# Top-10 indices of 8192 rows: each row spread over 16 partitions, sums of exponentials folded across partitions by one-hot matmuls, and candidates gathered as single columns

## The chip, the cores and the metric

One core of one Trainium2 chip. The metric is the time of one execution in device microseconds (us); medians of several executions are given. Trace views are of one profiled execution each. Lines such as L124 are lines of the kernel in question, so they differ between the two kernels. In the views PE is TensorE, PEld its weight loads, DVE VectorE, ACT ScalarE and POOL GpSimd; SPq and ACTq are the queues on which SyncE and ScalarE issue DMA transfers. PEclk is the TensorE clock that was granted; clock 1.00 is called warm below, 0.50 cold.

## The reference, cut to what matters

```python
def setup_inputs():
    return {"x": np.random.randn(8192, 8192).astype(np.float32), "k": 10}

def reference(x, k):
    indices = np.argpartition(x, -k, axis=1)[:, -k:]
    values = np.take_along_axis(x, indices, axis=1)
    sorted_idx = np.argsort(-values, axis=1)
    return np.take_along_axis(indices, sorted_idx, axis=1)
```

The input is 8192 x 8192 x 4 bytes = 268.4 MB. The output is small: ten 64-bit indices a row.

## The kernel before

The kernel takes 128 rows at a time (a tile; 64 of them). ScalarE computes steep exponentials of the whole row, TensorE adds them up over chunks of eight neighbouring elements, VectorE finds the twelve chunks with the largest sums, GpSimd gathers the elements of those chunks, TensorE sorts the gathered pieces to their rows, and VectorE ranks the 96 candidates. A final check falls back to a slow exact branch if the twelve chunks could have missed something.

```python
C = 8; NCHUNK = N // C; G = 12; PER = 6; HALF = NCHUNK // 2; LAG = 2     # (cut)

def load(t):                     # partition p holds row t*128 + p; 2 pieces of 16 KB a partition (8 of 4 KB for tile 0)
    ...
def weigh(t):
    for h in range(2):
        e = epool.tile([P, HALF, C], bf16, tag="e", name="e")
        nc.scalar.activation(out=e..., in_=xt[:, h * H:(h + 1) * H], func=ACTF.Exp, ...)
        for w in range(C):
            nc.tensor.matmul(ss[t][:, h, :], lhsT=eye, rhs=e[:, :, w],     # every eighth bf16
                             start=w == 0, stop=w == C - 1)

def choose(t):                   # max / max_index / match_replace / max / max_index over 1024 sums, then the indices
    ...
def gather(t):
    for a in range(G // PER):    # two instructions; 16 x 6 indices each, a run of 8 elements per index
        runs = gws[t][:, :, a * PER:(a + 1) * PER, :].rearrange("p r s w -> p s r w")
        nc.gpsimd.add_instruction(mybir.InstIndirectCopy(..., num_valid_indices=16 * PER))

def extract(t):                  # each partition's own row out of the 16 rows gathered in its group
    for r in range(16):
        nc.tensor.matmul(gs[t], lhsT=own[:, r, :], rhs=gw[:, r, :, :]..., start=r == 0, stop=r == 15)

# (cut) schedule: weigh(0), weigh(1); then per t: choose(t), gather(t), weigh(t+2), extract(t), load(t+3), rank(t-2)
```

A GpSimd gather applies the same list of indices to a whole group of 16 partitions: the trace shows it writing 128x768, 96 runs of 8 elements in every partition, of which six are its own row's. In this kernel the 16 partitions hold 16 different rows, so of every run that is gathered only one partition in 16 holds something that is wanted, and the matmuls with masked identities throw the rest away.

## Time and profile before

| | before |
|---|---|
| median time | 1342.99 us |
| TensorE busy | 1309.0 us (98%) |
| of a tile's 20.5 us: chunk sums / extraction | 14.4 / 6.1 us |
| GpSimd per tile, two gathers | 4.8 us for one; 9.8 us from when the indices are ready to when the extraction may start |
| loads | 268.4 MB at a mean of 202 GB/s |

The lines that carry this stand in the prediction. Two more rows of the page, each with one value for each fortieth of the span, show the granted TensorE clock in tenths and the rate of the DMA engines:

```profile
PEclk9956556566565565565665655655656656556556
...
GB/s 396 315 231 218 229 156 244 208 168 251 184 194 250 163 213 235 159 235 212 165 250 191 188 250 164 214 236 156 235 213 166 251 189 187 251 151 227 126 0 3
```

The DMA row starts near 400 GB/s while the first buffers fill and then sinks to about 200, because each load waits for a buffer that TensorE's pace sets free (SyncE's queue waits 1059.7 us, 60 times, for the gather that ends a buffer's use, and the gather waits for the sums). This is what a hidden transfer looks like: it could go twice as fast.

### The profile page before, as it was taken

The page shows a single profiled execution, that of the slowest core. Times are in us where ns is not written, and L with a number is a line of the kernel's source. Part 1 is how long each engine was busy: PE and PEld are TensorE (multiplying, and loading weights), DVE is VectorE, ACT ScalarE, POOL GpSimd, SP SyncE. Part 2 cuts the span into 40 slices and gives each one's busy share as a digit, 9 for nine tenths or more (in the row PEclk, how much of TensorE's full clock was granted, in tenths as well). Part 3 has the DMA queues.
Part 4 walks back from the last instruction along what each step waited for, and adds up shares of the span by engine and source line. Part 5 has one row for each costly group of instructions (what it writes and reads, how often), then busy time and mean ns, then how long its engine had stood idle before and what let it go on. Part 6 is the DMA issues. An engine that isn't in the chain of part 4 may idle for free.

```text
span 1341.3 us, 8449 instructions
## 1 busy us (share of the span) xinstructions
PE 1309.0 (98%) x3074; PEld 526.6 (39%) x3074; DVE 527.7 (39%) x1208; ACT 488.2 (36%) x258; POOL 147.0 (11%) x135
## 2 busy tenths in 40 slices
PE   5999999999999999999999999999999999999995
PEld 0234434434344344344343343442443433434424
DVE  0524325334254244343353342542434433434424
ACT  5433433433334334334334333343343343333410
POOL 0111110110111111101101101111111011011110
PEclk9956556566565565565665655655656656556556
DMA  9755546546446455455465464554554644645300
GB/s 396 315 231 218 229 156 244 208 168 251 184 194 250 163 213 235 159 235 212 165 250 191 188 250 164 214 236 156 235 213 166 251 189 187 251 151 227 126 0 3
DMA packets 27945, 270.75 MB, mean 202 GB/s; under 512 B 10496, under 2 KB 10624, under 8 KB 11648
## 3 DMA queue, kind: packets, MB, share of 16 engines
q1 hardware_dynamic: 27616, 269.10, 50.1%
q10 hardware_dynamic: 288, 1.11, 0.2%
q8 instruction: 24, 0.39, 0.1%
q14 instruction: 17, 0.14, 0.0%
HBM read 269.55 MB, written 0.66 MB: 201 GB/s over the span
## 4 chain that ended last, share of the span: by engine, by line
PE 98%; DMA 1%; issue 0%; ACT 0%; DVE 0%; POOL 0%; SPq 0%; ACTq 0%
PE s L124 69%; PE g L168 29%; DMA xt<-in_x_dram 1%; ACT e L118 0%; POOL gw L154 0%; ACT L118 0%; SPq L80 0%; DVE hot L198 0%; DVE hot L202 0%; DVE posb L182 0%; DVE posb L179 0%; DVE pick L206 0%; DVE t8a L178 0%; DVE t8b L181 0%; DVE ngood L245 0%
## 5 line engine op out<-in xcount | busy, mean ns | idle before, releaser
L124 PE MATMUL s<-e,eye 128*128 128x512 bf16 x1024 | 931.6, 1077 | 16.3 <-ACT e L118 16.3
L118 ACT ACTIVATE e<-xt,bias 128x4096 bf16<-128x4096 f32 x128 | 474.7, 3708 | 786.1 <-issue 779.4
L168 PEld LDWEIGHTS g<-gw,own 128*128 128x128 f32 x2048 | 407.1, 304 | 91.5 <-issue 84.5
L124 PEld LDWEIGHTS <-eye 128*128 128x128 bf16 x1024 | 125.9, 124 | 713.8 <-issue 709.4
L168 PE MATMUL g<-gw,own 128*128 128x96 f32 x2048 | 398.3, 387 | 6.8 <-POOL gw L154 6.8
L136 DVE MAX8 wall<-s 128x8 f32<-128x1024 f32 x64 | 78.9, 1233 | 770.8 <-PE s L124 770.8
L154 POOL INDIRECT_COPY gw<-xt,idx 128x768 f32 x128 | 146.3, 1143 | 1177.6 <-issue 1010.2
L141 DVE MAX8 wall<-m 128x8 f32<-128x1024 f32 x64 | 78.6, 1228 | 2.2
L137 DVE FIND_INDEX8 cidb<-wall,s 128x8 uint16<-128x1024 f32 x64 | 78.3, 1223 | 0.0
L142 DVE FIND_INDEX8 cidb<-wall,m 128x8 uint16<-128x1024 f32 x64 | 78.0, 1219 | 0.0
L139 DVE MATCH_REPLACE8 m<-wall,s 128x1024 f32<-128x1024 f32 x64 | 77.7, 1214 | 0.0
L118 ACT ACTIVATION_READ_ACCUMULATOR e<-xt,bias 128x1 f32 x128 | 23.9, 186 | 0.0
L178 DVE MAX8 t8a<-g 128x8 f32<-128x96 f32 x64 | 16.6, 259 | 13.4 <-PE g L168 13.4
L234 ACT ACTIVATE e<-tall,bias 128x64 f32<-128x64 f32 x1 | 0.3, 348 | 48.5 <-DVE tall L183 48.5
L181 DVE MAX8 t8b<-g 128x8 f32<-128x96 f32 x64 | 16.7, 261 | 2.2
L179 DVE FIND_INDEX8 posb<-t8a,g 128x8 uint16<-128x96 f32 x64 | 16.4, 257 | 0.0
L182 DVE FIND_INDEX8 posb<-t8b,g 128x8 uint16<-128x96 f32 x64 | 16.1, 252 | 0.0
L180 DVE MATCH_REPLACE8 g<-t8a,g 128x96 f32<-128x96 f32 x64 | 15.8, 247 | 0.0
L144 DVE TENSOR_SCALAR idx<-cidb 128x12 uint16<-128x12 uint16 x64 | 10.9, 171 | 7.4 <-DVE cidb L142 0.9
L198 DVE TENSOR_TENSOR hot<-slot,slots 128x960 f16<-128x960 uint16 x8 | 9.3, 1167 | 0.0
L206 DVE TENSOR_REDUCE pick<-hot 128x80 f32<-128x960 f16 x8 | 9.2, 1152 | 0.2
L183 DVE COPY tall<-t8b 128x1 f32<-128x1 f32 x64 | 8.6, 134 | 0.0
(27 smaller groups left out, 47.9 us busy)
## 6 DMA issues: line engine op xcount, KB each, us to landing
xt<-in_x_dram SPq DMA_DIRECT2D x126, 2048.0 KB, 11.7
xt<-in_x_dram SPq DMA_DIRECT2D x8, 512.0 KB, 9.2
own<-topk_own ACTq DMA_DIRECT2D x1, 1024.0 KB, 7.2
out_dram<-opack SPq DMA_DIRECT2D x8, 80.0 KB, 3.1
eye_f<-topk_eye ACTq DMA_DIRECT2D x1, 64.0 KB, 3.3
```

Source lines behind the costliest of these rows:

```text
L118: nc.scalar.activation(out=e.rearrange("p c w -> p (c w)"), in_=xt[:, h * H:(h + 1) * H], func=ACTF.Exp, bias=bias[:, 0:1], scale=BETA, ac ...
L124: nc.tensor.matmul(ss[t][:, h, :], lhsT=eye, rhs=e[:, :, w], start=w == 0, stop=w == C - 1)
L136: nc.vector.max(out=w16[:, 0:8], in_=m)
L137: nc.vector.max_index(out=cid[:, 0:8], in_max=w16[:, 0:8], in_values=m)
L139: nc.vector.match_replace(out=m2, in_to_replace=w16[:, 0:8], in_values=m, imm_value=-1.0)
L141: nc.vector.max(out=w16[:, 8:16], in_=m2)
L142: nc.vector.max_index(out=cid[:, 8:16], in_max=w16[:, 8:16], in_values=m2)
L154: nc.gpsimd.add_instruction(mybir.InstIndirectCopy(name=nc.get_next_instruction_name(), ins=[nc.gpsimd.lower_ap(xts[t]), nc.gpsimd.lower_a ...
L168: nc.tensor.matmul(gs[t], lhsT=own[:, r, :], rhs=gw[:, r, :, :].rearrange("p s w -> p (s w)"), start=r == 0, stop=r == 15)
L178: nc.vector.max(out=t8a, in_=g)
L179: nc.vector.max_index(out=pos[:, 0:8], in_max=t8a, in_values=g)
L181: nc.vector.max(out=t8b, in_=g2)
```

## The change

The intent is to read the exponentials in the order in which they lie. A row is cut into 16 parts of 512 elements which lie in 16 neighbouring partitions; a chunk is then one column of 16 elements, one in each of those partitions. Sums across partitions are what a matmul does: sixteen one-hot weight tiles (`group`) fold the parts of eight rows each into the 128 output rows. A gather of one index now brings 16 wanted elements, one in each partition. They arrive in the wrong direction, so each gathered column is multiplied with a mask (`spread`) and turned back by a matmul (`extract`). The core of the diff, with cuts marked:

```diff
-        for w in range(C):
-            nc.tensor.matmul(ss[t][:, h, :], lhsT=eye, rhs=e[:, :, w], start=w == 0, stop=w == C - 1)
+        for i in range(SP_):
+            s = h * SP_ + i
+            nc.tensor.matmul(ss[t], lhsT=group[:, s, :], rhs=e[:, i, :], start=s == 0, stop=s == S - 1)
 # ... load: 2 KB runs instead of rows
+        src = x[t * P:(t + 1) * P, :].rearrange("(s a) (q j) -> (a q) s j", a=A, q=R)
+        for s in range(0, S, S // 4):
+            nc.sync.dma_start(out=dst[:, s:s + S // 4, :], in_=src[:, s:s + S // 4, :])
 # ... choose over 512 sums instead of 1024; one gather of 16 x 12 single elements instead of two of 16 x 6 runs of 8
+    def spread(t):
+        nc.vector.tensor_tensor(out=masked[t], in0=cands.pop(t)..., in1=own..., op=ALU.mult)     # 128 x 1536
     def extract(t):
-        for r in range(16): nc.tensor.matmul(gs[t], lhsT=own[:, r, :], rhs=gw[:, r, :, :]..., ...)
+        for c in range(G):
+            nc.tensor.matmul(gs[t][:, c, :], lhsT=mk[:, c, :, :]..., rhs=place, start=True, stop=True)
 # ... rank over 192 candidates instead of 96, its six steps interleaved with the six of choose; LAG 3
+    def store(b):                # results of 8 tiles: eight stores from ScalarE's queue (before: one from SyncE's)
+        for a in range(A):
+            nc.scalar.dma_start(out=out_atn[a, :, b * TB:(b + 1) * TB, :], in_=o[a * S:(a + 1) * S, :, :])
 # ... schedule per t: choose(t) with rank(t-3), gather(t), weigh(t+1), store, spread(t-1), extract(t-1), decode, load(t+3)
```

More of the change, by code (lines that the diff above doesn't have):

```diff
@@ L12 @@
 N = 8192
-C = 8
-NCHUNK = N // C
+R = 16
+A = P // R
+S = P // A
+W = N // R
 KMAX = 10
 G = 12
-PER = 6
-HALF = NCHUNK // 2
+PIECES = 2
+SP_ = S // PIECES
 TB = 8
@@ L24 @@
 BIG_NEG = -1e30
-LAG = 2
+LAG = 3
 @with_exitstack
@@ L52 @@
     out_u32 = out.bitcast(u32)
-    out_tpn = out_u32.rearrange("(t p) n -> p t n", p=P)
+    out_atn = out_u32.rearrange("(t s a) n -> a s t n", s=S, a=A)
     consts = ctx.enter_context(tc.tile_pool(name="consts", bufs=1))
     epool = ctx.enter_context(tc.tile_pool(name="e", bufs=3))
-    gwpool = ctx.enter_context(tc.tile_pool(name="gw", bufs=2))
     small = ctx.enter_context(tc.tile_pool(name="small", bufs=2))
@@ L64 @@
     gpsum = ctx.enter_context(
-        tc.tile_pool(name="gpsum", bufs=2, space=bass.MemoryType.PSUM)
+        tc.tile_pool(name="gpsum", bufs=3, space=bass.MemoryType.PSUM)
     )
@@ L69 @@
     )
-    xts, es, ss, gs, idxs, gws, batch = {}, {}, {}, {}, {}, {}, {}
-    H = N // 2
+    xts, ss, gs, idxs, cands, masked, batch, ready = {}, {}, {}, {}, {}, {}, {}, {}
     def load(t):
         xts[t] = xpool.tile([P, N], fp32, tag="xt", name="xt")
-        r0 = t * P
-        nparts = 8 if t == 0 else 2
-        w = N // nparts
-        for h in range(nparts):
-            nc.sync.dma_start(
-                out=xts[t][:, h * w:(h + 1) * w], in_=x[r0:r0 + P, h * w:(h + 1) * w]
-            )
+        src = x[t * P:(t + 1) * P, :].rearrange("(s a) (q j) -> (a q) s j", a=A, q=R)
+        dst = xts[t].rearrange("p (s j) -> p s j", j=W)
+        n = S // 4
+        for s in range(0, S, n):
+            nc.sync.dma_start(out=dst[:, s:s + n, :], in_=src[:, s:s + n, :])
     for t in range(3):
         load(t)
+    part = np.arange(P)
+    own_np = (part[:, None] // R == np.arange(A)[None, :]).astype(np.float32)
+    place_np = (part[:, None] % R == np.arange(R)[None, :]).astype(np.float32)
+    base_np = ((part % S) * W).astype(np.float32)[:, None]
+    cpack_np = np.concatenate([own_np, place_np, base_np], axis=1)
+    cpack_dram = nc.inline_tensor(np.ascontiguousarray(cpack_np), name="topk_cpack")
+    cpack = consts.tile([P, A + R + 1], fp32)
+    nc.scalar.dma_start(out=cpack, in_=cpack_dram.ap())
+    own, place, base = cpack[:, 0:A], cpack[:, A:A + R], cpack[:, A + R:A + R + 1]
     bias = consts.tile([P, 1], fp32)
@@ L90 @@
     nc.vector.memset(ones, 1.0)
-    eye_np = np.eye(P, dtype=np.float32)
-    eye_dram = nc.inline_tensor(eye_np, name="topk_eye")
-    eye_f = consts.tile([P, P], fp32)
-    nc.scalar.dma_start(out=eye_f, in_=eye_dram.ap())
-    eye = consts.tile([P, P], bf16)
-    nc.vector.tensor_copy(out=eye, in_=eye_f)
-    own_np = np.stack([np.diag((np.arange(P) % 16 == r).astype(np.float32)) for r in range(16)], 1)
-    own_dram = nc.inline_tensor(np.ascontiguousarray(own_np).reshape(P, 16 * P), name="topk_own")
-    own = consts.tile([P, 16, P], fp32)
-    nc.scalar.dma_start(out=own.rearrange("p r q -> p (r q)"), in_=own_dram.ap())
+    group = consts.tile([P, S, P], bf16)
+    nc.vector.memset(group, 0.0)
+    for s in range(S):
+        nc.vector.tensor_copy(
+            out=group[:, s, :].rearrange("p (a s) -> p a s", s=S)[:, :, s], in_=own
+        )
     slots_i = consts.tile([P, G], i32)
@@ L107 @@
     tall = consts.tile([P, ntiles], fp32)
-    eall = consts.tile([P, ntiles, 2], fp32)
+    eall = consts.tile([P, ntiles, PIECES], fp32)
     opacks = [consts.tile([P, TB, KMAX, 2], u32, name=f"opack{i}") for i in range(2)]
@@ L114, in weigh @@
         xt = xts[t]
-        ss[t] = spsum.tile([P, 2, HALF], fp32, tag="s", name="s")
-        for h in range(2):
-            e = epool.tile([P, HALF, C], bf16, tag="e", name="e")
+        ss[t] = spsum.tile([P, W], fp32, tag="s", name="s")
+        for h in range(PIECES):
+            e = epool.tile([P, SP_, W], bf16, tag="e", name="e")
             nc.scalar.activation(
-                out=e.rearrange("p c w -> p (c w)"), in_=xt[:, h * H:(h + 1) * H],
+                out=e.rearrange("p s j -> p (s j)"),
+                in_=xt[:, h * SP_ * W:(h + 1) * SP_ * W],
                 func=ACTF.Exp, bias=bias[:, 0:1], scale=BETA,
@@ L122, in weigh, with choose_steps @@
             )
-            for w in range(C):
-                nc.tensor.matmul(ss[t][:, h, :], lhsT=eye, rhs=e[:, :, w],
-                                 start=w == 0, stop=w == C - 1)
-    def choose(t):
-        m = ss.pop(t).rearrange("p h c -> p (h c)")
+            for i in range(SP_):
+                s = h * SP_ + i
+                nc.tensor.matmul(ss[t], lhsT=group[:, s, :], rhs=e[:, i, :],
+                                 start=s == 0, stop=s == S - 1)
+    def choose_steps(t):
+        m = ss.pop(t)
         if t % TB == 0:
@@ L135, in choose @@
         w16 = wall[:, t, :]
-        nc.vector.max(out=w16[:, 0:8], in_=m)
-        nc.vector.max_index(out=cid[:, 0:8], in_max=w16[:, 0:8], in_values=m)
-        m2 = small.tile([P, NCHUNK], fp32, tag="m2")
-        nc.vector.match_replace(out=m2, in_to_replace=w16[:, 0:8], in_values=m,
-                                imm_value=-1.0)
-        nc.vector.max(out=w16[:, 8:16], in_=m2)
-        nc.vector.max_index(out=cid[:, 8:16], in_max=w16[:, 8:16], in_values=m2)
-        idxs[t] = small.tile([P, G // PER, 8], u16, tag="idx", name="idx")
@@ L144, in choose @@
-        nc.vector.tensor_scalar(
-            out=idxs[t][:, :, 0:PER],
-            in0=cid[:, 0:G].rearrange("p (a b) -> p a b", b=PER),
-            scalar1=float(NCHUNK - 1), scalar2=float(C), op0=ALU.min, op1=ALU.mult,
-        )
-    def gather(t):
-        gws[t] = gwpool.tile([P, 16, G, C], fp32, tag="gw", name="gw")
-        for a in range(G // PER):
-            runs = gws[t][:, :, a * PER:(a + 1) * PER, :].rearrange("p r s w -> p s r w")
-            nc.gpsimd.add_instruction(
-                mybir.InstIndirectCopy(
-                    name=nc.get_next_instruction_name(),
-                    ins=[nc.gpsimd.lower_ap(xts[t]), nc.gpsimd.lower_ap(idxs[t][:, a, 0:PER])],
-                    outs=[nc.gpsimd.lower_ap(runs)],
-                    num_valid_indices=16 * PER,
-                )
-            )
-        del xts[t], idxs[t]
@@ L164, in extract @@
-    def extract(t):
-        gw = gws.pop(t)
-        gs[t] = gpsum.tile([P, G * C], fp32, tag="g", name="g")
-        for r in range(16):
-            nc.tensor.matmul(gs[t], lhsT=own[:, r, :],
-                             rhs=gw[:, r, :, :].rearrange("p s w -> p (s w)"),
-                             start=r == 0, stop=r == 15)
-    def rank(t):
-        g = gs.pop(t)
-        pos = batch[t // TB][1][:, t % TB, :]
-        t8a = small.tile([P, 8], fp32, tag="t8a")
-        t8b = small.tile([P, 8], fp32, tag="t8b")
-        g2 = small.tile([P, G * C], fp32, tag="g2")
-        nc.vector.max(out=t8a, in_=g)
-        nc.vector.max_index(out=pos[:, 0:8], in_max=t8a, in_values=g)
-        nc.vector.match_replace(out=g2, in_to_replace=t8a, in_values=g, imm_value=BIG_NEG)
-        nc.vector.max(out=t8b, in_=g2)
-        nc.vector.max_index(out=pos[:, 8:16], in_max=t8b, in_values=g2)
-        nc.vector.tensor_copy(out=tall[:, t:t + 1], in_=t8b[:, KMAX - 9:KMAX - 8])
-        if t % TB == TB - 1:
-            decode(t // TB)
+        m2 = small.tile([P, W], fp32, tag="m2", name="m2")
@@ new lines, in choose_steps @@
+        idxs[t] = small.tile([P, G], u16, tag="idx", name="idx")
+        return [
+            lambda: nc.vector.max(out=w16[:, 0:8], in_=m),
+            lambda: nc.vector.match_replace(out=m2, in_to_replace=w16[:, 0:8], in_values=m,
+                                            imm_value=-1.0),
+            lambda: nc.vector.max_index(out=cid[:, 0:8], in_max=w16[:, 0:8], in_values=m),
+            lambda: nc.vector.max(out=w16[:, 8:16], in_=m2),
+            lambda: nc.vector.max_index(out=cid[:, 8:16], in_max=w16[:, 8:16], in_values=m2),
+            lambda: nc.vector.tensor_scalar(
+                out=idxs[t], in0=cid[:, 0:G], scalar1=float(W - 1), scalar2=base,
+                op0=ALU.min, op1=ALU.add,
+            ),
+        ]
@@ new lines, in gather @@
+    def gather(t):
+        cands[t] = small.tile([P, G, S], fp32, tag="cand", name="cand")
+        nc.gpsimd.add_instruction(
+            mybir.InstIndirectCopy(
+                name=nc.get_next_instruction_name(),
+                ins=[nc.gpsimd.lower_ap(xts[t]), nc.gpsimd.lower_ap(idxs[t])],
+                outs=[nc.gpsimd.lower_ap(cands[t].rearrange("p g s -> p (g s)"))],
+                num_valid_indices=S * G,
+            )
+        )
+        del xts[t], idxs[t]
+    def spread(t):
+        shape = [P, G, A, S]
+        masked[t] = small.tile(shape, fp32, tag="masked", name="masked")
+        nc.vector.tensor_tensor(
+            out=masked[t], in0=cands.pop(t).unsqueeze(2).to_broadcast(shape),
+            in1=own.unsqueeze(1).unsqueeze(3).to_broadcast(shape), op=ALU.mult,
+        )
@@ new lines, in extract, with rank_steps @@
+    def extract(t):
+        mk = masked.pop(t)
+        gs[t] = gpsum.tile([P, G, R], fp32, tag="g", name="g")
+        for c in range(G):
+            nc.tensor.matmul(gs[t][:, c, :], lhsT=mk[:, c, :, :].rearrange("p a s -> p (a s)"),
+                             rhs=place, start=True, stop=True)
+    def rank_steps(t):
+        g = gs.pop(t).rearrange("p c q -> p (c q)")
+        pos = batch[t // TB][1][:, t % TB, :]
+        t8a = small.tile([P, 8], fp32, tag="t8a", name="t8a")
+        t8b = small.tile([P, 8], fp32, tag="t8b", name="t8b")
+        g2 = small.tile([P, G * R], fp32, tag="g2", name="g2")
+        return [
+            lambda: nc.vector.max(out=t8a, in_=g),
+            lambda: nc.vector.match_replace(out=g2, in_to_replace=t8a, in_values=g,
+                                            imm_value=BIG_NEG),
+            lambda: nc.vector.max_index(out=pos[:, 0:8], in_max=t8a, in_values=g),
+            lambda: nc.vector.max(out=t8b, in_=g2),
+            lambda: nc.vector.max_index(out=pos[:, 8:16], in_max=t8b, in_values=g2),
+            lambda: nc.vector.tensor_copy(out=tall[:, t:t + 1],
+                                          in_=t8b[:, KMAX - 9:KMAX - 8]),
+        ]
@@ L190, in decode @@
         low = bpool.tile([P, TB, KMAX], u16, tag="low")
-        nc.vector.tensor_scalar(out=slot, in0=posb[:, :, 0:KMAX], scalar1=C.bit_length() - 1,
+        nc.vector.tensor_scalar(out=slot, in0=posb[:, :, 0:KMAX], scalar1=R.bit_length() - 1,
                                 scalar2=None, op0=ALU.logical_shift_right)
-        nc.vector.tensor_scalar(out=low, in0=posb[:, :, 0:KMAX], scalar1=C - 1,
+        nc.vector.tensor_scalar(out=low, in0=posb[:, :, 0:KMAX], scalar1=R - 1,
                                 scalar2=None, op0=ALU.bitwise_and)
@@ L208, in decode @@
         nc.vector.scalar_tensor_tensor(
-            out=o[:, :, :, 0], in0=pick, scalar=float(C), in1=low, op0=ALU.mult, op1=ALU.add,
+            out=o[:, :, :, 0], in0=low, scalar=float(W), in1=pick, op0=ALU.mult, op1=ALU.add,
         )
-        nc.sync.dma_start(
-            out=out_tpn[:, b * TB:(b + 1) * TB, :],
-            in_=o.rearrange("p t k two -> p t (k two)"),
-        )
+        ready[b] = o
+    def store(b):
+        o = ready.pop(b).rearrange("p t k two -> p t (k two)")
+        for a in range(A):
+            nc.scalar.dma_start(
+                out=out_atn[a, :, b * TB:(b + 1) * TB, :], in_=o[a * S:(a + 1) * S, :, :]
+            )
     with tc.manual_schedule():
         weigh(0)
-        weigh(1)
         for t in range(ntiles + LAG):
+            first = choose_steps(t) if t < ntiles else []
+            second = rank_steps(t - LAG) if t >= LAG else []
+            for i in range(6):
+                for steps in (first, second):
+                    if steps:
+                        steps[i]()
             if t < ntiles:
-                choose(t)
                 gather(t)
-                if t + 2 < ntiles:
-                    weigh(t + 2)
-                extract(t)
-                if t + 3 < ntiles:
-                    load(t + 3)
-            if t >= LAG:
-                rank(t - LAG)
+                if t + 1 < ntiles:
+                    weigh(t + 1)
+            for b in list(ready):
+                store(b)
+            if 1 <= t <= ntiles:
+                spread(t - 1)
+                extract(t - 1)
+            if t >= LAG and (t - LAG) % TB == TB - 1:
+                decode((t - LAG) // TB)
+            if t + 3 < ntiles:
+                load(t + 3)
+        for b in list(ready):
+            store(b)
     e10 = small.tile([P, ntiles], fp32, tag="e10")
     nc.scalar.activation(out=e10, in_=tall, func=ACTF.Exp, bias=bias[:, 0:1], scale=BETA)
-    good = small.tile([P, 3, ntiles], fp32, tag="good")
+    good = small.tile([P, 1 + PIECES, ntiles], fp32, tag="good")
     nc.vector.tensor_scalar(
-        out=good[:, 0:2, :].rearrange("p a t -> p (a t)"),
+        out=good[:, 0:PIECES, :].rearrange("p a t -> p (a t)"),
         in0=eall.rearrange("p t a -> p (t a)"), scalar1=FINITE, scalar2=None, op0=ALU.is_lt,
@@ L240 @@
     nc.vector.scalar_tensor_tensor(
-        out=good[:, 2, :], in0=e10, scalar=SLACK, in1=wall[:, :, G],
+        out=good[:, PIECES, :], in0=e10, scalar=SLACK, in1=wall[:, :, G],
         op0=ALU.mult, op1=ALU.is_gt,
@@ L249 @@
     nc.vector.tensor_copy(out=ngood, in_=gps)
-    checks = P * 3 * ntiles
+    checks = P * (1 + PIECES) * ntiles
     passed = nc.values_load(ngood[0:1, 0:1], min_val=0, max_val=checks)
```

## The prediction

> **What bounds the kernel now.** I read the page's engine shares first, then the chain that ended last, then the costliest groups, and then four closer views: TensorE's timeline in the middle of the run, the windows at the start and the end, GpSimd's timeline at the end, and ScalarE's at the start.
>
> ```profile
> PE 1309.0 (98%) x3074; PEld 526.6 (39%) x3074; DVE 527.7 (39%) x1208; ACT 488.2 (36%) x258; POOL 147.0 (11%) x135
> ...
> PE 98%; DMA 1%; issue 0%; ACT 0%; DVE 0%; POOL 0%; SPq 0%; ACTq 0%
> PE s L124 69%; PE g L168 29%; DMA xt<-in_x_dram 1%; ACT e L118 0%; POOL gw L154 0%; ACT L118 0%; SPq L80 0%; DVE hot L198 0%; DVE hot L202 0%; DVE posb L182 0%; DVE posb L179 0%; DVE pick L206 0%; DVE t8a L178 0%; DVE t8b L181 0%; DVE ngood L245 0%
> ...
> L118 ACT ACTIVATE e<-xt,bias 128x4096 bf16<-128x4096 f32 x128 | 474.7, 3708 | 786.1 <-issue 779.4
> ...
> L137 DVE FIND_INDEX8 cidb<-wall,s 128x8 uint16<-128x1024 f32 x64 | 78.3, 1223 | 0.0
> ...
> L179 DVE FIND_INDEX8 posb<-t8a,g 128x8 uint16<-128x96 f32 x64 | 16.4, 257 | 0.0
> ```
>
> TensorE is busy 98% and is 98% of the chain; every other engine is below 40%. The timeline of TensorE alone (start, length, what) gives the rhythm:
>
> ```profile
> 597.98 14.56 PE L124 MATMUL s<-e,eye 128*128 128x512 bf16 x16
> 612.36 6.26 PE L168 MATMUL g<-gw,own 128*128 128x96 f32 x32
> 618.46 14.56 PE L124 MATMUL s<-e,eye 128*128 128x512 bf16 x16
> ```
>
> One tile of 128 rows takes 618.46 - 597.98 = 20.5 us: 14.4 us of chunk sums (16 matmuls, 900 ns each from start to start; the 1077 ns of the group is a modelled end that overlaps the next) and 6.1 us of extraction (32 records, 191 ns each; the program has 16 fp32 matmuls there, so each is two passes). 64 x 20.5 = 1311 us, and the rest is start and tail. The DMA load of 268.4 MB (8192 x 8192 x 4 bytes) hides: the page's mean is 202 GB/s, while windows of 3 us at the start show what the queue can do. Their columns are busy times of PE, PEld, DVE, ACT and POOL, granted TensorE clock, DMA share, GB/s:
>
> ```profile
> 6.00:9.00 3.00, 0.00 (x0) 0.00 (x0) 0.00 (x0) 0.00 (x0) 0.00 (x0) 1.00 1.00 414
> 9.00:12.00 3.00, 0.00 (x0) 0.00 (x0) 0.00 (x0) 0.89 (x1) 0.00 (x0) 1.00 1.03 416
> ...
> 24.00:27.00 3.00, 3.00 (x4) 0.38 (x3) 0.00 (x0) 1.80 (x3) 0.00 (x0) 1.00 1.01 431
> ...
> 1308.70:1312.00 3.30, 3.30 (x17) 3.30 (x16) 3.07 (x5) 0.00 (x0) 0.00 (x0) 0.50 0.00 0
> 1315.00:1318.50 3.50, 3.50 (x32) 3.35 (x30) 1.79 (x11) 0.00 (x0) 0.00 (x0) 1.00 0.00 0
> ```
>
> The first two are mostly the first tile's 4 KB rows, the third 16 KB rows. The last two are extraction alone, at granted clock 0.50 (3.30/17 = 194 ns a pass) and 1.00 (3.50/32 = 109 ns).
>
> GpSimd's 11% misleads. At the end of the run its two gathers of a tile read:
>
> ```profile
> 1319.34 1.15 POOL L154 INDIRECT_COPY gw<-xt,idx 128x768 f32 x1 [14.55 <-PE g L168]
> 1324.13 1.15 POOL L154 INDIRECT_COPY gw<-xt,idx 128x768 f32 x1 [3.64 <-issue]
> ```
>
> Their indices were ready at 1315.5 (the index instruction starts at 1315.36 and lasts 0.17), and the extraction that waits for the second starts at 1325.32. So one gather of 96 runs of 8 elements takes 4.8 us, of which the record shows the last 1.15, and a tile's two take 9.6 us.
>
> **What the Trainium skill says.** "SBUF — State Buffer", section on the DMA port swizzle: SBUF lines are 16 bytes and an access that moves to a new line each time is penalised. The chunk sums read every eighth bf16, one element per line. The trace agrees: 900 ns for 512 columns both in the first 58 us at granted clock 1.00 (48 matmuls in 43.36 us) and later near 0.5, so the read and not the clock sets it. "TensorE: Matmul & The Clock Gate", section "Back-to-back issue gap": about N/1.2 ns cold and N/2.4 + 2.5 ns warm, so 427 and 216 ns for 512 contiguous columns; no run here shows it yet. "DMA: Bandwidth & Descriptors", section "Why small descriptors are slow (HBM only)": a fixed cost per packet; the 415 against 431 GB/s above agrees. "GPSIMD Engine Reference", section "Key points": GpSimd contends with VectorE instructions that have two SBUF inputs; no run shows it here.
>
> **The change part by part**, per tile.
>
> TensorE, sums: still 16 matmuls of 512 columns, but each now reads 512 adjacent bf16, and weights differ (16 one-hot matrices; their loads took 124 ns and lie beside the matmul before). 16 x 216 = 3.5 us warm, 16 x 427 = 6.8 us cold, for 14.4. Extraction: 12 fp32 matmuls of 16 columns, 24 passes instead of 32. At 194 and 109 ns as an upper bound 4.7 or 2.6 us; with 80 columns fewer I guess 3.3 or 1.8. TensorE: 5.3 to 10.1 us for 20.5.
>
> VectorE, choice over 512 instead of 1024 sums: FIND_INDEX8 went from 257 ns at 96 elements to 1223 at 1024, 1.04 ns an element, so 690 ns at 512, 357 at 192. Five passes of about 690, three value loads (92, 92, 72) and the 171 ns index step: 3.9 us. Ranking over 192 instead of 96: 5 x 357 + 256 + 134 = 2.2 us. New masking, 1536 fp32 products: the mixed-type product of 960 elements took 1167 ns, so about 1.04 x 1536 + 170 = 1.77 us. Decoding is unchanged in size: one decode per 8 tiles is 1.16 + 0.65 + 1.15 + about 0.6 = 3.6 us, so 0.5 us a tile. Sum 8.4 us: as much in total as now (8.2), but for a far shorter period.
>
> ScalarE: unchanged, two halves at 3.78 us from start to start (12.41 to 16.19): 7.6 us. It also issues 8 result stores per batch of 8 tiles at about 0.4 us each (its two issues at the start took 0.36 and 0.45): 0.4 us. Sum 8.0 us.
>
> GpSimd: one gather of 192 single elements instead of two of 96 runs of 8. If the cost goes by index, 192 x 50 ns = 9.6 us; if by element moved, 4.8 x 192/768 = 1.2 us. I take 7 us, nearer the first[...].
>
> DMA: the same bytes in 2 KB runs, 131,072 packets instead of some 17,000 of 4 or 16 KB. Per engine (a sixteenth): 4 KB in 4096/25.9 = 157.9 ns, 16 KB in 16384/26.9 = 609.6 ns; hence 7.3 ns a packet plus 27.2 bytes a ns. A 2 KB packet is 75.3 + 7.3 = 82.6 ns, 397 GB/s in all. An estimate from two windows: 10.56 us a tile, 268.4 MB/397 = 676 us.
>
> So the loads are the longest of five (DMA 10.6, TensorE up to 10.1, VectorE 8.4, ScalarE 8.0, GpSimd about 7), and they become the bound. Can four x buffers feed them? A buffer is held from issue to gather's end: about 2 us latency, 10.6 transfer, 3.9 for the second half on ScalarE, up to 3.4 for its matmuls, 6.1 for choice with ranking interleaved, 7 for the gather: 33 us, below 4 x 10.56 = 42. Yes, with 9 us to spare.
>
> Added on the path: start 3 us; tail after the last byte 3.9 + 2.5 + 6.1 + 7 + 1.8 (mask) + 2.7 (extraction) + 2.2 (rank) + 8 (decode, check and store, as now from 1333.4 to 1341.3) = 34 us. Result stores now share the pool of 8 DMA semaphores with the loads, as the built program's waits show: a store waits for loads still in flight, and later loads wait for stores. I give each of 8 batches 2.5 us, a quarter of a tile's load: 20 us. Sum 676 + 3 + 34 + 20 = 733; I say 735 us.
>
> **The rivals.** First, GpSimd becomes the bound: 9.6 us by index, plus 1.77 when the two-input masking, which runs as the next gather starts, shuts it out, is 11.4 us a tile, 728 + 40 = about 770 us. For it: 50 ns per run as measured. Against: seven of eight elements of each run are gone. Second, waits in a ring: TensorE must finish extraction of tile t-1, which waits for masking, which stands behind the choice of tile t, before the sums of t+2. Two periods must hold 6.1 + 1.8 + 3.3 + 6.8 plus some 1 us of semaphores, 19 us cold, so 9.5 us: under 10.56, but it adds to any late gather; 12 us a tile would be 810. Third, DMA holds the 415 GB/s of 4 KB rows and stores hide: 647 + 37 = 684 us. Fourth, strided 2 KB rows are much slower than the estimate (330 GB/s): 813 + 37 = 850 us.
>
> **Range and chances.** The first and second rival together have some 30%, the fourth 10%, the third 15%. Range 685 to 815. No engine sum comes near 20 us a tile, so faster by over 2% is 0.99, within 2% 0.005, slower 0.005.
>
> **What would show it.** Right: DMA share above 9 tenths throughout, GB/s near 390, ScalarE's waits ended by x loads, sum matmuls 216 to 427 ns apart. First rival: masking waits for the gather, DMA share near 8, gathers back to back. Second: DMA has gaps and x loads wait for gathers while GpSimd idles. Store coupling: a DMA dip every eighth tile. What would make it wrong altogether: strided sums slow for another reason than the 16-byte step, or a gather over 15 us.

## The result and the profile after

| | before | after |
|---|---|---|
| median of 4 executions | 1342.99 us | 725.35 us (723.2 to 726.48) |
| ratio | 1 | 0.540 (95% interval 0.5386 to 0.5413) |
| TensorE busy | 1309.0 us (98%) | 541.0 us (75%) |
| VectorE / ScalarE busy | 527.7 / 488.2 us | 456.9 / 488.2 us |
| loads | 202 GB/s | 374 GB/s |

A ratio is the mean time of one kernel's fast runs over that of the other's of the same rounds, so it is not quite the ratio of the medians.

From the page of the changed kernel, the rows that answer to those shown before (engine shares, DMA and GB/s by slice, the chain by engine, and groups):

```profile
PE 541.0 (75%) x2562; PEld 323.0 (45%) x2562; DVE 456.9 (63%) x1288; ACT 488.2 (68%) x258; POOL 65.6 (9%) x71
...
DMA  9999999999999999999999999999999999999900
...
GB/s 336 409 407 409 407 408 407 406 333 408 407 409 346 395 407 408 408 353 409 407 409 407 345 406 409 407 405 358 408 408 407 348 402 408 408 409 338 382 1 6
...
SPq 77%; DMA 16%; issue 3%; DVE 1%; PE 1%; ACT 1%; POOL 0%; DVEq 0%; ACTq 0%
...
L124 ACT ACTIVATE e<-xt,bias 128x4096 bf16<-128x4096 f32 x128 | 474.7, 3709 | 192.3 <-DMA xt<-in_x_dram 169.4
...
L132 PE MATMUL s<-e,group 128*128 128x512 bf16 x1024 | 359.8, 517 | 163.4 <-ACT e L124 163.4
...
L183 PE MATMUL g<-cpack,masked 128*128 128x16 f32 x1536 | 195.8, 273 | 5.2 <-DVE masked L174 5.2
...
L161 POOL INDIRECT_COPY cand<-xt,idx 128x192 f32 x64 | 64.9, 1014 | 635.9 <-issue 438.7
...
L174 DVE TENSOR_TENSOR masked<-cand,cpack 128x1536 f32<-128x1536 f32 x64 | 111.9, 1748 | 2.6 <-POOL cand L161 2.6
```

The DMA row is at 9 tenths in every slice up to the tail, and GB/s stands mostly at 405 to 409 except for a dip in every fifth slice or so. The chain, which was TensorE for 98%, is now SyncE's queue (the issuing of loads, each after an earlier one has landed) and loads themselves, 93% together. ScalarE's idle time is now ended by loads (169.4 of 192.3 us). And VectorE gains little: the durations of all its groups add up to 8.2 us a tile, before to 8.7 (the busy rows, 456.9 and 527.7 us, count overlaps once), since the masking of 1748 ns takes what the shorter rows give.

Four windows show the matmuls at both clocks (columns as in the prediction: busy time with counts for PE, PEld, DVE, ACT, POOL, then granted clock, DMA share, GB/s). The first two lie in chunk sums, the last two in extraction:

```profile
346.20:350.20 4.00, 4.00 (x11) 1.40 (x11) 1.85 (x3) 2.74 (x3) 0.00 (x0) 0.50 1.05 409
354.40:355.90 1.50, 1.50 (x9) 0.68 (x7) 1.50 (x7) 1.43 (x1) 0.00 (x0) 1.00 1.06 407
341.20:345.90 4.70, 4.70 (x24) 4.70 (x23) 4.50 (x16) 3.31 (x3) 0.13 (x1) 0.50 1.05 409
351.80:354.20 2.40, 2.40 (x25) 2.40 (x24) 2.32 (x8) 1.32 (x2) 0.63 (x1) 1.00 1.05 409
```

At clock 0.50 the sums go at about 427 ns from start to start and at 1.00 at 216 ns (eight of them take 1.89 us to the modelled end of the last); the trace so agrees with the formula of the Trainium skill, "TensorE: Matmul & The Clock Gate", section "Back-to-back issue gap", which the prediction could not yet test. Its other figure there does not hold here: about 131 ns a matmul of 512 columns in a stream of weight loads and matmuls, where this trace shows 216 at best. Whole extractions of 24 passes around these windows last 5.14 and 2.75 us in TensorE's timeline; from start to start a pass takes 213 and 112 ns. (A count in a window takes in passes that are cut by its edges, so a window's length over its count comes out too low.)

The timeline gives the gather's true length. Its indices are ready when the index step ends; its record shows only its last microsecond:

```profile
346.12 0.21 DVE L153 TENSOR_SCALAR idx<-cidb,cpack 128x12 uint16<-128x12 uint16 x1
...
346.31 1.74 DVE L174 TENSOR_TENSOR masked<-cand,cpack 128x1536 f32<-128x1536 f32 x1
...
351.42 1.01 POOL L161 INDIRECT_COPY cand<-xt,idx 128x192 f32 x1 [10.09 <-issue]
```

It runs from 346.33 to 352.43, 6.1 us. The masking of the tile before lies in its first 1.75 us; the 63 gathers with a masking at their start took 6.0 to 7.5 us. The first gather of the run, with no masking beside it, took 4.65 us (indices at 24.34, end at 28.99).

The dips have an owner. In the list of what SyncE's queue waited for (total, times, longest):

```profile
SPq L83 <- DMA out_dram<-opack: 64.2, 7, 9.6
```

Seven times, once for each batch but the last, a load waited up to 9.6 us for result stores to finish. One such wait, in windows (columns as above), and the queue that carries the stores (packets, MB, share of the 16 DMA engines' span):

```profile
138.00:142.00 4.00, 3.23 (x12) 1.24 (x12) 4.00 (x12) 3.20 (x1) 0.00 (x0) 0.60 1.05 410
145.00:147.00 2.00, 2.00 (x15) 1.53 (x13) 0.98 (x4) 2.00 (x1) 1.02 (x1) 0.85 0.79 99
...
q10 hardware_dynamic: 9360, 0.67, 0.9%
```

In the trace's instruction records a store issued at 139.3 us and the load issued at 144.6 count on the same semaphore, so the load had to wait; by then the loads issued earlier had nearly run out, and the rate fell from 410 to 99 GB/s. The stores' own packets explain less: their queue takes 0.9% of the span, 6.5 us in all, which is little beside the 17.4 us that the stores turn out to cost below.

### The profile page after: what moved, and what is told of

Same layout as the page of the kernel before. It is cut to its first block, busy times and chain, and to the rows that moved or that the text cites. A ratio compares the mean times of both kernels' runs of the same rounds, so it can differ in the third digit from the quotient of the medians.

```text
span 721.4 us, 7720 instructions
## 1 busy us (share of the span) xinstructions
PE 541.0 (75%) x2562; PEld 323.0 (45%) x2562; DVE 456.9 (63%) x1288; ACT 488.2 (68%) x258; POOL 65.6 (9%) x71
## 4 chain that ended last, share of the span: by engine, by line
SPq 77%; DMA 16%; issue 3%; DVE 1%; PE 1%; ACT 1%; POOL 0%; DVEq 0%; ACTq 0%
SPq L83 77%; DMA xt<-in_x_dram 16%; PE g L183 1%; ACT e L124 1%; PE s L132 0%; DVE masked L174 0%; DVE hot L214 0%; POOL cand L161 0%; DVE g L194 0%; DVE wall L147 0%; DVE posb L196 0%; DVE cidb L150 0%; DVE m L148 0%; DVE t8a L193 0%; DVE hot L218 0%
## 5 line engine op out<-in xcount | busy, mean ns | idle before, releaser
L124 ACT ACTIVATE e<-xt,bias 128x4096 bf16<-128x4096 f32 x128 | 474.7, 3709 | 192.3 <-DMA xt<-in_x_dram 169.4
L132 PE MATMUL s<-e,group 128*128 128x512 bf16 x1024 | 359.8, 517 | 163.4 <-ACT e L124 163.4
L132 PEld LDWEIGHTS <-group 128*128 128x128 bf16 x1024 | 129.6, 129 | 367.4 <-issue 322.6
L183 PEld LDWEIGHTS g<-cpack,masked 128*128 128x128 f32 x1536 | 203.8, 211 | 18.9 <-issue 10.7
L147 DVE MAX8 wall<-s 128x8 f32<-128x512 f32 x64 | 44.8, 699 | 248.5 <-PE s L132 248.4
L183 PE MATMUL g<-cpack,masked 128*128 128x16 f32 x1536 | 195.8, 273 | 5.2 <-DVE masked L174 5.2
L161 POOL INDIRECT_COPY cand<-xt,idx 128x192 f32 x64 | 64.9, 1014 | 635.9 <-issue 438.7
L174 DVE TENSOR_TENSOR masked<-cand,cpack 128x1536 f32<-128x1536 f32 x64 | 111.9, 1748 | 2.6 <-POOL cand L161 2.6
L150 DVE FIND_INDEX8 cidb<-wall,s 128x8 uint16<-128x512 f32 x64 | 44.1, 689 | 0.0
L152 DVE FIND_INDEX8 cidb<-wall,m 128x8 uint16<-128x512 f32 x64 | 43.8, 684 | 0.0
L148 DVE MATCH_REPLACE8 m<-wall,s 128x512 f32<-128x512 f32 x64 | 43.5, 680 | 0.0
```

What stands on the lines that cost most here:

```text
L124: nc.scalar.activation(out=e.rearrange("p s j -> p (s j)"), in_=xt[:, h * SP_ * W:(h + 1) * SP_ * W], func=ACTF.Exp, bias=bias[:, 0:1], sc ...
L132: nc.tensor.matmul(ss[t], lhsT=group[:, s, :], rhs=e[:, i, :], start=s == 0, stop=s == S - 1)
L147: lambda: nc.vector.max(out=w16[:, 0:8], in_=m),
L148: lambda: nc.vector.match_replace(out=m2, in_to_replace=w16[:, 0:8], in_values=m, imm_value=-1.0),
L150: lambda: nc.vector.max_index(out=cid[:, 0:8], in_max=w16[:, 0:8], in_values=m),
L152: lambda: nc.vector.max_index(out=cid[:, 8:16], in_max=w16[:, 8:16], in_values=m2),
```

## The experiments

The experiments could not use the gather instruction itself. All of them use plain GpSimd copies in its place, which read the same x buffer after the same indices and write the same candidate buffer. Their results are therefore wrong, and the exact branch at the end is switched off so that it does not run. Eleven kernels ran, three rounds each; the kernel before, run beside them, took 1342.3 to 1343.5 us.

**Control: the stand-in.**

```diff
-        nc.gpsimd.add_instruction(mybir.InstIndirectCopy(... xts[t], idxs[t] ... num_valid_indices=S * G))
+        nc.gpsimd.tensor_copy(out=cands[t][:, :, 0], in_=idxs[t])
+        for i in range(9):
+            nc.gpsimd.tensor_copy(out=cands[t]..., in_=xts[t][:, i * G * S:(i + 1) * G * S])
-    with tc.If(passed < checks):
+    with tc.If(passed < 1):
```

> The changed kernel with its gather replaced by ten plain GpSimd copies of the same tiles (one of the indices, nine of 192 elements of x), so the result is wrong on purpose and the final repair branch is never taken. It is the control for the other runs. Loads-bound theory: the stand-in is no longer than a tile's load of 10.3 us, so the time stays at 725 us within 1.5%, and the DMA share stays at 9 tenths. Gather-bound or ring-bound theory: the time follows the length of the stand-in, whatever it turns out to be (shorter than the gather's 6.1 us: below 710; longer: above 740).

Measured: 725.81 us, within 0.1% of the changed kernel. GpSimd's timeline in it:

```profile
356.23 1.72 POOL L161 CAST cand<-idx 128x12 f32<-128x12 uint16 x1 [4.28 <-DVE tall L196]
358.01 3.61 POOL L163 COPY cand<-xt 128x192 f32<-128x192 f32 x9
```

Ten copies take 5.4 us. The first, of only 12 elements, lasts 1.72 us because the masking runs on VectorE at that time (it lasts 1.75); in a run below where the two don't meet the same copy takes 0.21 us. The control stands for the changed kernel in what follows.

**Packet size, both ways.** Same bytes and the same four transfers a tile, in 8 KB runs (wrong rows) and in 1 KB runs (right data):

```diff
-            nc.sync.dma_start(out=dst[:, s:s + n, :], in_=src[:, s:s + n, :])                   # 2 KB runs
+            nc.sync.dma_start(out=xts[t][:, s:s + n], in_=x[t * P:(t + 1) * P, s:s + n])        # 8 KB runs
# or
+            for c in range(0, W, W // 2):                                                       # 1 KB runs, n doubled
+                nc.sync.dma_start(out=dst[:, s:s + n, c:c + W // 2], in_=src[:, s:s + n, c:c + W // 2])
```

> The control loading each partition's 8192 elements in four 8 KB runs of one row instead of sixteen 2 KB runs (wrong rows, same bytes, same count and size of transfers). Loads-bound theory with a fixed cost per packet (27.2 bytes per ns an engine and 5 ns a packet, which is what 408 GB/s at 2 KB gives): 8 KB packets take 306 ns, 428 GB/s, 627 us of load instead of 658, so about 695 us if the control is 725. If another engine or ring binds at 10.3 us a tile: no change.

> The control loading in 1 KB runs (each 2 KB run as two, data in the right place; still four transfers of 1 MB a tile). With 5 ns a packet: 42.6 ns per 1 KB, 384 GB/s, 699 us of load, so about 766 us if the control is 725. With the 7.3 ns of the prediction: 365 GB/s, 735 us of load, about 800. If packets cost nothing, or if loads don't bind: no change.

Measured: 697.74 us and 756.37 us, against 725.81. The GB/s rows of the two, 8 KB first:

```profile
GB/s 369 428 425 427 425 428 425 401 359 426 425 429 342 428 425 425 430 342 428 426 428 425 339 427 426 426 407 369 424 428 427 339 424 427 426 427 347 387 1 6
```

```profile
GB/s 327 386 385 386 385 386 384 384 352 386 381 381 352 380 384 385 385 353 386 385 386 385 348 385 386 385 382 354 386 384 385 323 379 386 385 386 352 377 2 6
```

The expectation for 1 KB, about 766 us, was 10 us too high. The plateaus are about 427 and 385 GB/s, and 408 in the control. An engine moves a sixteenth: 8192/26.7, 2048/25.5 and 1024/24.06 give 307, 80.3 and 42.6 ns a packet. From 1 to 2 KB that is 27.1 bytes a ns, and what is left is 4.8 ns a packet; it gives 307 ns at 8 KB, as measured. The time follows the loads in both directions, by 28 and 31 us where the loads alone (268.4 MB over the plateau's rate) change by 29 and 39: with the slower loads part of the stores' cost disappears in them (the dips are shallower, 352 out of 385, and loads waited for stores for 38.1 us in all, in the control for 65.5). So the loads bound the kernel, and they do so with a fixed cost per packet. The 8 KB run also changes which row goes to which partition; that it falls on the line of the two others speaks for the packet as the cause.

**The gather's length, both ways.** One copy in place of nine, and 24.

> The control with one copy of 192 elements in the gather's place instead of nine: GpSimd's work per tile falls from about 5.4 us (1.7 of them shut out by the masking) to about 2.2 us. Loads-bound theory: only the tail gets shorter, by the 3.2 us of the last tile's gather: 722 us, within 1% of the control's 725.8. Gather-bound or ring-bound theory: up to 3 us a tile, 530 us or anything clearly below 715.

> The control with 24 copies instead of nine: 24 x 0.40 + 1.7 = 11.4 us on GpSimd per tile, the very figure of the prediction's first rival (9.6 us by index plus the masking that shuts GpSimd out). If that rival had been true of the gather the kernel would look like this: 64 x 11.4 = 730 us from the first gather at 24 us to the last, plus some 30 us of tail: 780 to 790 us, GpSimd back to back, DMA with gaps. If something else keeps GpSimd and the loads apart, it stays below 760.

Measured: 723.75 us and 785.85 us. Three us less for GpSimd in each of 64 tiles are worth 2 us in all. They were expected in the last tile, but the traces do not show them there: from the start of the last exponential to the end are 36.5 us (685.5 to 722.0), in the control 35.3 (687.8 to 723.1). Where the 2 us come from stays open. With 11.4 us a tile GpSimd takes over; the chain by engine and GpSimd's timeline of that run:

```profile
POOL 70%; DMA 12%; issue 9%; SPq 4%; ACTq 1%; DVE 1%; ACT 1%; PE 1%; POOLq 0%; DVEq 0%
```

```profile
311.77 0.21 POOL L161 CAST cand<-idx 128x12 f32<-128x12 uint16 x1
312.04 11.24 POOL L163 COPY cand<-xt 128x192 f32<-128x192 f32 x24
```

Copies follow each other with no gap (11.24 us plus 0.21 a tile), and this is the number that the first rival named. The gather of 6.1 us lies far from it.

**The 16-byte step alone, put back.** Everything of the change stays, but the sums read their operand with a step of eight bf16 (wrong sums):

```diff
-                nc.tensor.matmul(ss[t], lhsT=group[:, s, :], rhs=e[:, i, :], ...)
+                nc.tensor.matmul(ss[t], lhsT=group[:, s, :],
+                                 rhs=e.rearrange("p s j -> p (s j)").rearrange("p (j w) -> p j w", w=SP_)[:, :, i], ...)
```

> The control with the sums' moving operand read with a step of 8 elements (16 bytes), as the kernel before reads it, and all else of the change in place (wrong sums). Line theory (the 16-byte step alone makes a matmul take 900 ns): 16 x 900 = 14.4 us of sums and 24 passes of 109 to 214 ns = 2.6 to 5.1 us of extraction, 17 to 19.5 us a tile, so 1130 to 1300 us, TensorE at 97%. If the sums of the kernel before were slow for another reason (one weight tile, PSUM), it stays near 726.

Measured: 1268.2 us, 0.945 of the kernel before. TensorE's timeline of it:

```profile
617.92 5.12 PE L180 MATMUL g<-cpack,masked 128*128 128x16 f32 x24
622.88 14.56 PE L132 MATMUL s<-e,group 128*128 128x512 bf16 x16
```

Sixteen sums take 14.4 us from start to start of what follows, exactly as in the kernel before, although weights, accumulation and PSUM layout are the changed kernel's. The step is the whole of the sums' loss. Only steps of one and of eight elements were run, so it is not shown that the 16-byte line is what matters, nor what a step of two or four costs.

**The 16-byte step alone, taken away from the kernel before.** First a control with copies of 9.5 us in the place of the two gathers, then one edit in it:

```diff
-                nc.tensor.matmul(ss[t][:, h, :], lhsT=eye, rhs=e[:, :, w], ...)
+                nc.tensor.matmul(ss[t][:, h, :], lhsT=eye, rhs=e.rearrange("p c w -> p (c w)")[:, w * HALF:(w + 1) * HALF], ...)
```

> The kernel before with its two gathers of a tile replaced by 24 plain GpSimd copies of about 9.5 us in all (wrong result on purpose). It is the control for the next run. TensorE bounds it, so the time stays at 1342 us within 1%.

> That control with one edit: each sum matmul reads 512 adjacent bf16 instead of every eighth (so the chunks are wrong, and eight elements of a chunk would lie 512 apart). Nothing else of the change. Theory that the gain is the 16-byte step alone: sums 3.5 to 6.8 us, extraction 3.5 to 6.2, so TensorE 7 to 13 us a tile, GpSimd 9.5, loads 268.4 MB at 428 GB/s 9.8, ScalarE 7.6: 10 to 12 us a tile, 690 to 810 us. If the change's other parts (one instead of two halves, fewer passes, the interleaved order, VectorE's shorter rows) are needed for the gain, it stays above 1000.

Measured: 1336.49 us for the control, 686.34 us with adjacent reads. It was expected between 690 and 810; it is a little faster, and faster than the changed kernel. TensorE's timeline, then the engine shares and GB/s of that run:

```profile
308.84 1.89 PE L124 MATMUL s<-e,eye 128*128 128x512 bf16 x8
...
313.82 3.71 PE L163 MATMUL g<-gw,own 128*128 128x96 f32 x32
```

```profile
PE 496.3 (73%) x3019; PEld 352.0 (51%) x3074; DVE 530.0 (77%) x1208; ACT 488.3 (71%) x258; POOL 533.4 (78%) x1543
...
GB/s 362 429 427 427 427 429 426 387 420 429 427 426 370 432 426 428 429 405 428 426 428 415 412 428 426 431 400 423 428 423 409 408 424 430 429 419 397 339 1 5
```

Eight sums now take 1.7 us instead of 7.2, TensorE is down to 73%, and with its 16 KB rows the kernel loads at about 427 GB/s between its dips. So one edit of an access pattern carries the whole gain, and more. It is not a valid kernel: with adjacent reads in that layout the eight elements of a chunk lie 512 apart in one partition, so a tile would need 8 x 192 = 1536 single indices for a group of 16 partitions. At the 4.65 us that 192 took, that would be some 37 us a tile of GpSimd, an estimate from the first gather of the changed kernel. Spreading the row over 16 partitions is the price for having both adjacent reads and one index for 16 wanted elements, and the price in time is the 2 KB packets.

**The stores.** All result stores at the end; then, in a second version, the first seven batches' after ScalarE's last exponentials and only the last batch's at the very end.

```diff
-    opacks = [consts.tile([P, TB, KMAX, 2], u32, name=f"opack{i}") for i in range(2)]
+    opack = consts.tile([P, ntiles, KMAX, 2], u32)
-            for b in list(ready): store(b)                    # every 8 tiles
+        store()                                               # version 1: behind the loop, all 64 tiles
# version 2: at t == ntiles - 1 store(0, ntiles - TB), behind the loop store(ntiles - TB, ntiles)
```

> The control with all result stores moved behind the last tile (64 stores of 10 KB become 8 of 80 KB), nothing else. Store-coupling theory: the dips of GB/s to about 345 in the slices of the batches go, and with them 8 x 2.7 us = about 20 us; the longer stores at the end give 2 to 3 us back: 705 to 710 us if the control is 725. Rival, the dips are something else (DRAM refresh, HBM bandwidth spent on writes): they stay and the time is that of the control within 4 us.

> As the run with all stores at the end, but the stores of the first seven batches are issued on ScalarE's queue after its last exponentials, when the loads have landed and 20 us of work are still to do, and only the last batch's stores wait for the last decode. Store-coupling theory: keeps the 18 us won in the load stage and saves the 9 us that the eight long stores cost at the end: 706 to 710 us. If the 18 us were not the stores' but the moved work's, it is no better than 716.6.

Measured: 716.62 us and 708.37 us, against 725.81. The first missed its expectation of 705 to 710, and its trace shows why:

```profile
697.84 9.06 ACTq L227 DMA_DIRECT2D out_dram<-opack  x8
```

The issue of eight long stores took 9.06 us on the path after the last decode, against some 3.9 us for eight short ones, and their completion follows. The load stage had become shorter as expected: the last exponential started at 668.7 us, in the control at 687.8. The second version keeps that (669.0) and moves most of the issue beside other work. Its GB/s row has no dip left:

```profile
GB/s 335 408 408 407 407 408 407 409 407 409 407 408 408 409 407 408 408 408 408 407 409 408 408 407 408 407 408 407 404 407 405 406 408 405 401 408 408 243 32 5
```

The stores cost 17.4 us of the changed kernel's time. No run kept them in the loop on semaphores of their own, so that the shared semaphores are the whole of it is not shown. The version has the stand-in, so it is no proof of a faster correct kernel, but it says what the next edit is.

**Three x buffers instead of four.**

> The control with three x buffers instead of four. The prediction's count of how long a buffer is held, with what was measured since put in: 2 us latency, 10.3 of transfer, 3.9 for the second half on ScalarE, 1.9 to 3.4 for its sums, 5.0 from the sums to the indices, 5.4 of gather: 28.5 to 30 us. Three buffers allow a tile every 9.5 to 10 us, still just below the 10.3 of the loads, so with the waits between engines I expect 730 to 760 us. If the true holding time is some 35 us: 11.7 us a tile, about 785. If much shorter: no change.

Measured: 752.6 us, in the expected range. What loads waited for in that run:

```profile
SPq L83 <- POOL cand L163: 374.8, 54, 9.4
```

Loads now wait for GpSimd's last copy of the buffer in 54 tiles, 374.8 us in all; with four buffers it was 20.6 us in 7 tiles. So the count of about 29 to 33 us of holding a buffer is near the truth, four buffers are enough and three are not.

## Why the prediction was right

It said 735 us in a range of 685 to 815, and 725.35 was measured. The bound and the waits were as it said. That the sum came so near is in part luck, because errors cancel: loads took 18 us less than it said and stores 3 less, start and tail some 8 more. Its steps one by one:

- **The new bound.** Loads are the longest of five: shown, by the DMA row, by the chain and by both packet runs. Their rate was estimated at 397 GB/s from 4 and 16 KB rows; it is 408. The packet's fixed cost was put at 7.3 ns and is 4.8; two early windows were too coarse for more. (Its 609.6 ns belong to 430 GB/s; with the 431 of the line shown it would have been 7.8 ns and 395 GB/s.) Loads take 658 us instead of 676.
- **The sums.** 900 ns became 427 or 216, with the clock, as estimated, and the step is the only cause, as both step runs show.
- **The extraction.** The guess of 1.8 to 3.3 us for 24 passes was too low: 2.75 to 5.14. A pass with 16 columns costs what one with 96 does: from start to start both take 213 ns where the clock is recorded at 0.50 and 112 at 1.00, so the fewer columns gained nothing. (The prediction's 194 and 109 were a window's length over its count.) With the sums TensorE needs 6.2 to 12.0 us of a 10.3 us tile. So the prediction's "up to 10.1" for a cold TensorE was too low, and cold it would need more than the loads' 10.3. At the mean clock of 0.755 that it got, it was busy for 8.5 us a tile (541.0/64) and did not bind.
- **VectorE, ScalarE.** 8.4 us a tile for VectorE was a sum of durations, which came to 8.2 (it compared this with 8.2 before, which is the busy row; the durations before are 8.7); ScalarE's 7.6 without stores is 488.2/64 as measured. Neither binds.
- **GpSimd.** 7 us were taken, a guess between two rules; 4.65 alone and 6.1 beside the masking were measured. The cost is neither by index (9.6) nor by element (1.2). The lockout that the first rival feared is real, 1.5 us a tile, but there was room for it. Of the second rival, waits in a ring, the sign is missing: SyncE's queue lists no wait of a load for a gather in the changed kernel.
- **The stores.** 20 us were given for the shared semaphores; taking the stores away from the load stage is worth 17.4.
- **Start and tail.** 34 us for the tail; from the start of the last exponential, which waits for the last load, at 685.3 to the end at 721.4 are 36.

The sum of the load stage, 658 us and some 18 of stores, leaves 9 us to the start of the last exponential at 685.3: the start (the first load packet moves at 1.9 us), the last landing, and what wasn't resolved.

One reading in the prediction was unsound, though its conclusion held. It took granted clock 1.00 in the first 58 us as proof that the slow sums don't follow the clock. But in that trace the first clock record begins at 64.8 us, and the strided run's trace holds none at all (its page has no PEclk row): a stretch without records is listed at 1.00. The pace tells as much: passes of 213 ns, those of clock 0.50, at the start of the extraction of 59.4 to 65.4 us and throughout the strided run. The records that do exist carry the conclusion. In the kernel before, 181 steps from one sum to the next lie where the clock is recorded at 1.00 and take 880 to 900 ns, and 673 lie at 0.50 and take 900. The adjacent sums of the changed kernel take 216 and 427 ns under the same two clocks.

## What to carry to other kernels

Look at the step of a matmul's moving operand before anything else: eight bf16 from one element to the next cost this kernel almost half its time (smaller steps were not tried), and the remedy is a data layout in which the sum runs across partitions. Then count what the layout costs where it meets memory: runs of 2 KB instead of 8 KB took 4% of the load rate, which only matters once loads are the bound. And when the transfers bind, small stores that share their completion semaphores with the loads are not free.

## What the Trainium skill lacked or had wrong

- "SBUF — State Buffer", section on the DMA port swizzle, says that crossing 16-byte lines costs, but not how much for TensorE: a bf16 moving operand with a step of 16 bytes takes 900 ns for 512 columns, against 427 or 216 ns with adjacent elements. The passage can be read as if a step of 8 bf16 were still free; here it was not.
- "DMA: Bandwidth & Descriptors", section "Why small descriptors are slow (HBM only)", has a cost in cycles and an example of 256 bytes; the runs show 4.8 ns a packet beside 27.1 bytes a ns an engine: 427, 408 and 385 GB/s at 8, 2 and 1 KB. No page says what it costs when loads and stores take turns on completion semaphores: with the stores moved away from the loads 17.4 us were gained here.
- "TensorE: Matmul & The Clock Gate", section "Back-to-back issue gap", gives about 131 ns a matmul of 512 columns in a stream of weight loads and matmuls; here such a stream takes 216 ns at best, which is the page's formula. The page has no figure for an fp32 pass with its own weights: 213 ns at clock 0.50 and 112 at 1.00, with 16 columns as with 96.
- "GPSIMD Engine Reference" has no figure for an indirect copy as a whole: 4.8 us for 96 runs of 8 elements a group of 16 partitions, 4.65 us for 192 single elements, 6.1 beside a VectorE product of two SBUF inputs. Its section "Performance pitfalls for Q7 kernels" puts a small read command, such as one per gather index, at about 102 cycles; at the page's 1.2 GHz that is some 16 us for 192, an estimate far above the measured 4.65. The contention with such a product is on the page ("Key points"); the runs add its size: a copy of 12 elements takes 1.72 us instead of 0.21.
- "TensorE: Matmul & The Clock Gate" warns that a trace's clock events can be unreliable. None of the pages consulted says that a granted clock of 1.00 can stand for a stretch without clock records: here the first 64.8 us of the kernel before and all of the strided run.
